# A linear-recurrence kernel (RWKV WKV): another timetable for the output stores, and one set of carry transfers on another queue

## Chip, cores and metric

The kernel runs on one core of a Trainium2 chip. The metric is the device time of one execution in microseconds (us); the median of three runs before the change is 285.42 us (284.81 to 285.78).

## What is computed

```python
for b in range(16):                      # batch; each of d_model = 256 channels on its own
    aa, bb, pp = 0, 0, -1e38
    for t in range(2048):
        ww = u + k[b, t]
        qq = maximum(pp, ww)
        e1, e2 = exp(pp - qq), exp(ww - qq)
        output[b, t] = (e1 * aa + e2 * v[b, t]) / (e1 * bb + e2 + 1e-08)
        ww = pp - w + k[b, t]
        qq = maximum(ww, k[b, t])
        e1, e2 = exp(ww - qq), exp(k[b, t] - qq)
        aa, bb, pp = e1 * aa + e2 * v[b, t], e1 * bb + e2, qq
```

A numerator and a denominator are carried along time with decay w, and each output is their quotient. Inputs k and v are 33.5 MB each, the output another 33.5 MB, all in 32-bit floats.

## The kernel before

Time is cut into 16 chunks of 128 steps, and the 16 batches into 4 groups of 4. A **tile** is one chunk of one group: 128 steps on the partitions, 4 x 256 channels along the free axis, 512 KB each of k, of v and of output. There are 64 tiles, numbered n = 4 c + p (chunk c, group p).

Within a tile the decayed sums are matrix products: the exponentials of k (two variants, one for each half of the recurrence) and their products with v lie in bf16 in a ring of 12 tiles, `EZR`, and TensorE multiplies them with triangular matrices: `den` (L357) makes the denominator, `num` (L375) the numerator. What a chunk inherits from the earlier ones is put into a row of each half of the tile, in the ring itself: these **carries** are worked out from sums over the chunk (`sums` to `state_next`, L250 to L333), turned by TensorE (`turn_back`, L336), copied to the small tile `cb` and written into the ring by four 8 KB transfers (`inject`, L343). `den` of the four tiles of a chunk can start only when its carries are in the ring.

The main loop goes through **slots**, n = 10 to 63 (after 10 slots that fill the pipeline). Slot n makes the exponentials of tile n, and for tile q = n - 10 the denominator and its reciprocal: ACT takes its logarithm into an output buffer (`den_log`, L363) and then exp of minus that (`den_exp`, L367). For the tile before, qp = n - 11, PE makes the numerators and DVE multiplies them in (`mult`, L379, two halves; the second is near the end of slot n). DVE also converts k (`round_k`, L190, of tile n + 2) and v (`cast_v`, L224) and multiplies exponentials with v (`times_v`, L231). After slot 63 a hand-written tail finishes tiles 53 to 63. Its first lines (L512 to L540) hold, in this order: `den(54)`, the stores that are left over, `den(55)`, the state of the last chunk, the store of tile 53, `den(56)` (the first that needs chunk 14's carries), `turn_back(15)`, and `inject(15)` on SyncE (SP). Then come tiles 54 to 63 one after the other; `den(60)` is the first that needs chunk 15's carries.

Every engine runs its instructions in the order in which they are written. SP issues all large transfers in such an order too: in each slot first `loads` (L79), usually v of one tile and k of the next, then `store` (L383) of as many tiles as the condition of L485 lets through. They share one hardware queue.

There are 19 data buffers of 512 KB, 8 of them for outputs at first. A list with due slots says which may be taken: a stored output's buffer is given back 4 slots after its store (`STORED`, L37, L386), which only sets the order; the real wait is a semaphore: `den_log` waits until the transfer that last read its buffer has landed. Where fewer than three output buffers are due, `loads` moves one over from the inputs (L81).

The condition in L485 gives, for tile m, a store in slot m + 14 up to slot 31, one slot later from 32, 44 and 56 on; from slot 59, when all is loaded, everything finished is stored at once (tiles 42 to 47 in that slot).

Carries go out on GpSimd's (POOL's) queue, except those of the last chunk, which SP issues.

Of the kernel before, what the change touches and what calls it, by code (L numbers as in the profile page):

```python
# [15 lines left out]
def kernel(  # L16
# [10 lines left out]
    PE, DVE, SC, POOL, SP = nc.tensor, nc.vector, nc.scalar, nc.gpsimd, nc.sync  # L27
# [4 lines left out]
    NST = T // TC  # L32
    D = 2 * Dm
    NP = 4 * NST
# [42 lines left out]
    loaded = 5  # L77

    def loads(slot):  # L79
        nonlocal loaded  # L80
        if slot + 2 >= LAG and sum(x <= slot + 2 for x, _ in free_out) < 3:  # L81
            free_out.append((slot + 2, take(slot, free)))
        while loaded < NP and loaded - slot < 9 and sum(x <= slot for x, _ in free) >= 2:
            load_v(loaded, slot)
            loaded += 1
            if loaded < NP:
                load_k(loaded, slot)
# [102 lines left out]
    def round_k(n, slot=0):  # L190
        km = consts.tile([128, 4, Dm], F32R, tag=f"km{n % 2}", name="km") if n < 2 else KM[n - 2]
        kr = kr_of.pop(n)
        K(DVE.tensor_copy(km, kr))  # L193
        free.append((slot, kr))
        KM[n] = km

    def logs(n):
        km = KM[n].rearrange("p (i n) d -> p i (n d)", i=2)

        def rows(q):  # L200
            for i in range(2):
                g = 32 * (2 * q + i)
                K(PE.matmul(half(n, q)[:, i, :], CO[g:g + 32, :],  # L203
                            WU[g:g + 32, :].unsqueeze(1).broadcast_to([32, 2, Dm]), start=True, stop=False,
                            tile_position=(g, 0), skip_group_check=True))

        def steps(q):
            for i in range(2):
                K(PE.matmul(half(n, q)[:, i, :], (NLE, NLZ)[q], km[:, i, :], start=False, stop=True,  # L209
                            skip_group_check=True))  # L210

        rows(0)
        rows(1)
        steps(0)
        steps(1)

    def exps(n):
        if n < TURNS:
            for q in range(2):
                K(SC.activation(ez(n)[:, q], half(n, q), ACT.Exp))  # L220
        else:
            K(SC.activation(ez(n)[:, 0:2], PS[:, 0:4, :].rearrange("p (q i) x -> p q i x", q=2), ACT.Exp))  # L222

    def cast_v(n, slot=0):  # L224
        vb = vbpool.tile([128, 4, Dm], BF16, tag="vb", name="vb")
        vr = vr_of.pop(n)
        K(DVE.tensor_copy(vb, vr))  # L227
        free.append((slot, vr))
        VB[n] = vb

    def times_v(n):  # L231
        vb = VB.pop(n).rearrange("p (i n) d -> p i (n d)", i=2)
        K(DVE.tensor_mul(ez(n)[:, 2:4], ez(n)[:, 0:2], vb.unsqueeze(1).broadcast_to([128, 2, 2, D])))  # L233
# [109 lines left out]
    def inject(c, queue=POOL):  # L343
        cb = small.tile([128, 128], BF16, tag="cb", name="cb")
        K(DVE.tensor_copy(cb, st.pop((c, "CT"))))  # L345
        r0 = 4 * c % RING
        for q in range(2):
            for h in range(2):
                r, x = HS * h + HS - 1, 32 * (2 * q + h)
                K(queue.dma_start(  # L350
                    out=EZR[r:r + 1, 2 * q, r0:r0 + 4, :, :].rearrange("o p i (b x) -> o (p i b) x", b=4),
                    in_=cb[x:x + 32, :]))
# [4 lines left out]
    def den(n, bank=DENB):  # L357
        for m, q in (("L", 0), ("Id", 1)):
            for i in range(2):
                K(PE.matmul(bank[:, i, :], mats[m], ez(n)[:, q, i, :], start=q == 0, stop=q == 1,  # L360
                            skip_group_check=True))
# [13 lines left out]
    def num(n, bank, i):  # L375
        for m, q in (("LN", 2), ("IdN", 3)):
            K(PE.matmul(bank, mats[m], ez(n)[:, q, i, :], start=q == 2, stop=q == 3, skip_group_check=True))  # L377

    def mult(n, bank, i):  # L379
        rd = RD[n]  # L380
        K(DVE.tensor_mul(rd[:, i, :], bank, rd[:, i, :]))  # L381

    def store(n, slot):  # L383
        rd = RD.pop(n).rearrange("p i (n d) -> p (i n) d", n=2)
        K(SP.dma_start(out=rows_of(out, n), in_=rd))
        free_out.append((slot + STORED, rd))  # L386

    later = {}
    for c in range(NST):
        s = 4 * c + 3  # L390
        plan = [(s + 1, "act" if s + 1 < LAG else "recip", copy_sums), (s + 1, "pe", turn),
                (s + 2, "act", state_logs), (s + 2, "mid", state_frames), (s + 2, "scan", state_scan), (s + 2, "scan", state_offsets),
                (s + 3, "recip", state_weights), (s + 3, "chain", state_chain),
                (s + 4, "nums", turn_back), (s + 4, "mid", inject), (s + 4, "mid", state_next)]
        if c == 0:
            plan = [(s + 1, "act", copy_sums), (s + 1, "pe", turn), (s + 1, "pe", state_logs),
                    (s + 1, "round", state_frames), (s + 1, "round", state_scan), (s + 1, "round", state_offsets),
                    (s + 2, "act", state_weights), (s + 2, "round", state_chain),
                    (s + 3, "pe", turn_back), (s + 3, "round", inject), (s + 3, "round", state_next)]
        if c == 1:  # L400
            plan = [(s + 1, "act", copy_sums), (s + 1, "pe", turn), (s + 2, "act", state_logs),
                    (s + 2, "round", state_frames), (s + 2, "round", state_scan), (s + 2, "round", state_offsets),
                    (s + 3, "recip", state_weights), (s + 3, "early", state_chain)] + plan[8:]
        if c == NST - 1:
            plan = []
        for slot, where, f in plan:
            later.setdefault((slot, where), []).append((f, c))

    def small_work(n, where):
        for f, c in later.pop((n, where), []):  # L410
            f(c)
# [35 lines left out]
    stored = 0  # L447

    def inverses(n):
        q, qp = n - LAG, n - LAG - 1  # L450
        if qp >= 0:
            num(qp, NUMB, 1)

        sums(n - 1)
        if n + 1 < NP:
            recip(q, lambda: small_work(n, "recip"))

    for n in range(LAG, NP):

        q, qp = n - LAG, n - LAG - 1  # L460
        if qp >= 0:
            num(qp, NUMB, 0)
        den(q)
        small_work(n, "nums")
        exps(n)
        small_work(n, "act")
        if qp >= 0:
            mult(qp, NUMB, 0)
        small_work(n, "mid")
        if n == LAG:  # L470

            inverses(n)
            small_work(n, "early")
        if n + 2 < NP:
            round_k(n + 2, n)

        if n % 4 in (3, 0):
            cast_v(n, n)
        if n + 1 == NP:
            times_v(n)  # L480
        elif n % 4 < 2:
            cast_v(n + 1, n)
        loads(n)

        while stored < (qp - 2 - max(0, n - 20) // 12 if loaded < NP else qp):  # L485
            store(stored, n)
            stored += 1
        if n > LAG:
            inverses(n)
        if qp >= 0:  # L490
            mult(qp, NUMB, 1)
        small_work(n, "scan")
        if n + 1 < NP:
            times_v(n)
            small_work(n, "chain")
            logs(n + 1)
        small_work(n, "pe")
# [4 lines left out]
    q, c = NP - LAG - 1, NST - 1  # L502
# [48 lines left out]
    n, p = NP - 1, (NP - 1) % 4  # L551
# [38 lines left out]
```

## Time and profile before

| | |
|---|---|
| time, median of 3 | 285.42 us |
| profiled span | 283.5 us |
| busy: DVE, PE, ACT, POOL | 261.1, 256.2, 253.6, 106.0 us |
| transfers | 67.12 MB read, 33.55 MB written |
| slot in the steady part | 15.9 us for 4 slots |
| 512 KB load or store, issue to landing | 8.0 to 8.2 us (median) |
| carry transfer of 8 KB, issue to landing | 5.3 us from POOL, 1.9 us from SP |

Read the page in three parts. Up to about 42 us the kernel fills its pipeline; up to about 254 us it runs the slots; then the tail. A high busy share over the whole span hides that: the parts have to be looked at one by one, and in each the question is which wait ends last.

### The profile page before, as it was taken

To read this page: it belongs to the slowest core of one execution; us is meant where nothing else is said; L and a number is where in the kernel's file an instruction comes from. 1 tells how busy PE (TensorE), PEld (TensorE's weight loads), DVE (VectorE), ACT (ScalarE), POOL (GpSimd) and SP (SyncE) were. 2 spreads that over 40 slices of the span, in tenths; PEclk is the share of its full clock that TensorE was granted. 3 is DMA by queue.
4 is the path that set the end of the run, shared out by engine and by line. 5 is a ranking of instruction groups with operands and counts; after the bars stand their busy time and mean duration, and the time that the engine had idled before them with its cause. 6 is when DMAs were issued, how large, how long until landed. Compare 5 with 4: busy or idle time off the path is not lost.

```text
span 283.5 us, 5049 instructions
## 1 busy us (share of the span) xinstructions
PE 256.2 (90%) x1662; PEld 119.5 (42%) x1694; DVE 261.1 (92%) x465; ACT 253.6 (89%) x252; POOL 106.0 (37%) x206
## 2 busy tenths in 40 slices
PE   6997896999999999999999999899999999997990
PEld 2444442544454444544454444444444344433430
DVE  4699989999999999999999999999999999987863
ACT  2576678999999999999999999899999999997991
POOL 7000424263445444253445445143546546242000
PEclk9999999999999999999999999999999999999997
DMA  6999999999999999999999999999999999999597
GB/s 225 349 348 350 348 331 350 333 348 352 384 375 382 384 381 385 383 382 382 384 377 384 375 384 377 378 376 369 382 379 384 383 384 378 380 384 334 167 340 252
DMA packets 103586, 101.54 MB, mean 358 GB/s; under 512 B 4284, under 2 KB 103560, under 8 KB 103560
## 3 DMA queue, kind: packets, MB, share of 16 engines
q1 hardware_dynamic: 101336, 100.45, 103.9%
q0 software_dynamic: 1920, 0.50, 0.8%
q8 instruction: 13, 0.21, 0.3%
q10 hardware_dynamic: 304, 0.27, 0.3%
q14 instruction: 13, 0.11, 0.1%
HBM read 67.12 MB, written 33.55 MB: 355 GB/s over the span
## 4 chain that ended last, share of the span: by engine, by line
DVE 35%; PE 27%; DMA 16%; ACT 9%; issue 9%; DVEq 1%; POOL 0%; ACTq 0%; POOLq 0%
DVE EZR L233 14%; DVE buf L381 11%; PE PS L377 9%; PE PS L209 9%; DMA buf<-in_k_dram 7%; DMA out_dram<-buf 6%; PE PS L257 3%; PE PS L203 3%; ACT EZR L222 3%; ACT buf L365 3%; DVE vb L227 3%; DVE km L193 3%; PE PS L360 2%; ACT buf L368 2%; DMA EZR<-cb 2%
## 5 line engine op out<-in xcount | busy, mean ns | idle before, releaser
L222 ACT ACTIVATE EZR<-PS 128x2048 bf16<-128x2048 f32 x54 | 101.2, 1874 | 3.3 <-PE PS L209 2.6
L381 DVE TENSOR_TENSOR buf<-PS,buf 128x512 f32<-128x512 f32 x128 | 87.6, 692 | 6.3 <-ACT buf L368 4.2
L233 DVE TENSOR_TENSOR EZR<-EZR,vb 128x2048 bf16<-128x2048 bf16 x64 | 78.3, 1224 | 3.1 <-ACT EZR L220 2.5
L365 ACT ACTIVATE buf<-PS 128x1024 f32<-128x1024 f32 x64 | 65.8, 1028 | 3.4 <-DMA out_dram<-buf 1.6
L368 ACT ACTIVATE buf<-buf 128x1024 f32<-128x1024 f32 (+1 forms) x65 | 67.9, 1049 | 0.9
L377 PE MATMUL PS<-EZR,LN 128*128 128x512 bf16 x128 | 48.8, 381 | 10.3 <-DVE buf L381 6.7
L350 POOL DMA_DIRECT2D EZR<-cb x60 | 36.7, 617 | 52.0 <-DVE cb L345 44.6
L209 PE MATMUL PS<-km,NLE 128*128 128x512 f32 x128 | 47.6, 454 | 1.8 <-DVE km L193 1.8
L193 DVE CAST km<-buf 128x1024 fp32r<-128x1024 f32 x64 | 44.2, 691 | 1.3 <-DMA buf<-in_k_dram 1.2
L227 DVE CAST vb<-buf 128x1024 bf16<-128x1024 f32 x64 | 43.3, 695 | 0.0
L377 PE MATMUL PS<-EZR,IdN 128*128 128x512 bf16 x112 | 42.4, 378 | 0.0
L209 PE MATMUL PS<-km,NLZ 128*128 128x512 f32 x128 | 41.0, 403 | 0.0
L360 PE MATMUL PS<-EZR,L 128*128 128x512 bf16 x128 | 38.1, 379 | 1.6 <-DMA EZR<-cb 1.6
L360 PE MATMUL PS<-EZR,Id 128*128 128x512 bf16 x115 | 35.3, 379 | 0.0
L288 POOL TENSOR_TENSOR F<-LL,LL 128x32 f32<-128x32 f32 x13 | 8.5, 654 | 63.6 <-ACT LL L279 63.6
L203 PE MATMUL PS<-WU,CO 32*128 32x512 bf16 x256 | 26.9, 393 | 2.7 <-DVE WU L421 1.6
L257 PE MATMUL PS<-EZR,OH 128*32 128x256 bf16 x512 | 26.2, 277 | 2.9 <-ACT LL L279 0.7
L209 PEld LDWEIGHTS PS<-km,NLZ 128*128 128x128 f32 x128 | 24.6, 192 | 5.7
L220 ACT ACTIVATE EZR<-PS 128x1024 bf16<-128x1024 f32 x20 | 19.4, 1020 | 8.4 <-PE PS L209 8.4
L209 PEld LDWEIGHTS PS<-km,NLE 128*128 128x128 f32 x128 | 19.4, 191 | 17.0 <-issue 12.9
L377 PEld LDWEIGHTS <-IdN 128*128 128x128 bf16 x128 | 12.5, 97 | 23.0 <-issue 20.8
L377 PEld LDWEIGHTS <-LN 128*128 128x128 bf16 x128 | 12.8, 100 | 18.3 <-issue 11.3
(71 smaller groups left out, 202.8 us busy)
## 6 DMA issues: line engine op xcount, KB each, us to landing
buf<-in_k_dram SPq DMA_DIRECT2D x64, 512.0 KB, 8.2
buf<-in_v_dram SPq DMA_DIRECT2D x64, 512.0 KB, 8.1
out_dram<-buf SPq DMA_DIRECT2D x63, 512.0 KB, 8.0
EZR<-cb POOLq DMA_DIRECT2D x60, 8.0 KB, 5.3
out_dram<-buf SPq DMA_DIRECT2D x2, 128.0 KB, 3.3
out_dram<-buf ACTq DMA_DIRECT2D x2, 128.0 KB, 3.2
EZR<-cb SPq DMA_DIRECT2D x4, 8.0 KB, 1.9
wuf<-in_w_dram ACTq DMA_DIRECT2D x1, 8.0 KB
```

Source lines behind the costliest of these rows:

```text
L193: K(DVE.tensor_copy(km, kr))
L203: K(PE.matmul(half(n, q)[:, i, :], CO[g:g + 32, :], WU[g:g + 32, :].unsqueeze(1).broadcast_to([32, 2, Dm]), start=True, stop=False, tile_p ...
L209: K(PE.matmul(half(n, q)[:, i, :], (NLE, NLZ)[q], km[:, i, :], start=False, stop=True, skip_group_check=True))
L222: K(SC.activation(ez(n)[:, 0:2], PS[:, 0:4, :].rearrange("p (q i) x -> p q i x", q=2), ACT.Exp))
L227: K(DVE.tensor_copy(vb, vr))
L233: K(DVE.tensor_mul(ez(n)[:, 2:4], ez(n)[:, 0:2], vb.unsqueeze(1).broadcast_to([128, 2, 2, D])))
L350: K(queue.dma_start(out=EZR[r:r + 1, 2 * q, r0:r0 + 4, :, :].rearrange("o p i (b x) -> o (p i b) x", b=4), in_=cb[x:x + 32, :]))
L360: K(PE.matmul(bank[:, i, :], mats[m], ez(n)[:, q, i, :], start=q == 0, stop=q == 1, skip_group_check=True))
L365: K(SC.activation(RD[n], bank, ACT.Ln, scale=RS))
L368: K(SC.activation(RD[n][:, i, :], RD[n][:, i, :], ACT.Exp, scale=-1.0))
L377: K(PE.matmul(bank, mats[m], ez(n)[:, q, i, :], start=q == 2, stop=q == 3, skip_group_check=True))
L381: K(DVE.tensor_mul(rd[:, i, :], bank, rd[:, i, :]))
```

## The change

```diff
-                (s + 4, "nums", turn_back), (s + 4, "mid", inject), (s + 4, "mid", state_next)]
+                (s + 4, "nums", turn_back), (s + 4, "mid", inject if c < NST - 2 else lambda c: inject(c, SP)),
+                (s + 4, "mid", state_next)]
...
-        while stored < (qp - 2 - max(0, n - 20) // 12 if loaded < NP else qp):
+        while stored < qp - (min(5, max(0, n - 18) // 5) if n < NP - 3 else 3):
             store(stored, n)
             stored += 1
```

The first edit concerns chunk 14 alone, the last that goes through this plan: its four carry transfers, in slot 63, are issued by SP and not by POOL. The second sets another timetable. Tile m is stored in slot m + 12, the first slot after its last `mult`, up to slot 22; from slots 23, 28, 33, 38 and 43 on each time one slot later, so from 43 on in slot m + 17. From slot 61 on the distance is m + 15. The buffers that outputs and loads use, and the points at which input buffers are moved over, follow from the new timetable. It is meant to give output buffers back in time, and to keep transfers that nothing waits for behind those that something waits for.

| stores | before | after |
|---|---|---|
| tile 0 | slot 14 | slot 12 |
| tile 10 | slot 24 | slot 22 |
| tile 15 | slot 29 | slot 29 |
| tile 25 | slot 40 | slot 41 |
| tile 39 | slot 55 | slot 56 |
| tiles 42 to 47 | slot 59 | slots 59 to 62 |
| tiles 48 to 51 | slots 60 to 63 | 48 in slot 63; 49 to 51 in the tail |

No instruction of PE, DVE or ACT is added, removed or moved; four transfer issues move from POOL to SP.

## The prediction

> **What bounds the kernel now.** I first read the page's slices and the chain by engine, to find the parts; then the windows, part by part; then the timeline around the waits.
>
> ```profile
> DVE  4699989999999999999999999999999999987863
> ACT  2576678999999999999999999899999999997991
> DMA  6999999999999999999999999999999999999597
> GB/s 225 349 348 350 348 331 350 333 348 352 384 375 382 384 381 385 383 382 382 384 377 384 375 384 377 378 376 369 382 379 384 383 384 378 380 384 334 167 340 252
> ...
> DVE 35%; PE 27%; DMA 16%; ACT 9%; issue 9%; DVEq 1%; POOL 0%; ACTq 0%; POOLq 0%
> ```
>
> One slice is 7.1 us. Up to slice 6 (42 us) transfers are full and DVE and ACT are not: loads bound the start. Then everything is full. Loads alone move at 349 GB/s, with stores among them at 380 to 384. From the issue list, two loads alone take 3.0 us, two loads with a store 4.1 us, against a slot of 3.97 us.
>
> ```profile
> core 0: us, PE busy (x) PEld busy (x) DVE busy (x) ACT busy (x) POOL busy (x), PEclk, DMA share, GB/s
> ...
> 119.00:135.00 16.00, 15.28 (x105) 7.24 (x106) 15.85 (x28) 15.82 (x16) 6.98 (x13) 1.00 1.09 382
> 135.00:151.00 16.00, 14.63 (x101) 6.82 (x101) 15.66 (x26) 15.19 (x15) 6.71 (x13) 1.00 1.09 381
> ...
> 167.00:183.00 16.00, 14.79 (x98) 6.84 (x99) 15.56 (x27) 15.20 (x16) 6.26 (x13) 1.00 1.09 378
> ...
> 262.50:269.00 6.50, 6.45 (x31) 2.96 (x31) 5.18 (x10) 6.50 (x8) 0.00 (x0) 1.00 0.48 157
> 269.00:283.50 14.50, 7.46 (x32) 2.96 (x31) 7.47 (x12) 8.27 (x10) 0.00 (x0) 0.88 0.88 298
> ```
>
> Up to 135 us DVE and ACT have under 0.2 us free in 16: they bound the slots, and a timetable of transfers can't speed them up. Between 135 and 199 us ACT loses some 0.6 us twice. The timeline of ACT names it: `den_log` waits for a store to give its buffer back.
>
> ```profile
> 142.29 1.03 ACT L365 ACTIVATE buf<-PS 128x1024 f32<-128x1024 f32 x1 [0.65 <-DMA out_dram<-buf]
> ...
> 178.50 1.03 ACT L365 ACTIVATE buf<-PS 128x1024 f32<-128x1024 f32 x1 [0.70 <-DMA out_dram<-buf]
> ```
>
> These are slots 35 and 44; smaller gaps lie before `den_log` in slots 34, 41, 45 and 49 (0.12, 0.22, 0.04, 0.22 us): 1.95 us on ACT in all. In the chain in order of time, `times_v` of equal slots starts at 122.35, 154.74 and 187.18 us; eight slots take 31.8 us undisturbed, so the path lost 0.59 and then 0.64 us. Then the tail:
>
> ```profile
> 253.95 2.05 POOL L350 DMA_DIRECT2D EZR<-cb  x4 [3.57 <-DVE cb L345]
> ...
> 260.10 0.59 PE L360 MATMUL PS<-EZR,L 128*128 128x512 bf16 x2 [1.55 <-DMA EZR<-cb]
> ...
> 261.16 1.02 ACT L365 ACTIVATE buf<-PS 128x1024 f32<-128x1024 f32 x1 [1.48 <-PE PS L360]
> ...
> 262.25 0.29 DVE L345 CAST cb<-PS 128x128 bf16<-128x128 f32 x1 [1.30 <-PE PS L339]
> ...
> 262.57 2.52 SPq L350 DMA_DIRECT2D EZR<-cb  x4
> ```
>
> POOL issues chunk 14's carries from 253.95 to 256.0, they land by about 260, and `den(56)`, ready at 258.55, waits 1.55 us. `turn_back(15)` and `inject(15)` queue behind it. From there ACT needs 1.86 us for a tile and sets the pace to the end. In 262.5 to 269 us transfers are half idle (157 GB/s): there is room there for stores that are put off.
>
> **What the Trainium skill says.** "DMA: Bandwidth & Descriptors", section "Queues, rings and completion order": a DMA engine takes one ring's descriptors in order and goes round-robin between rings. The trace agrees: SP's transfers land in the order of issue, 6.9 us after the end of issue when backlogged, and a small carry takes 5.3 us from POOL even beside that backlog, 1.9 us from SP with little in front. The same page, "Anatomy of one DMA": DMA engines do not wait on semaphores, the issuing sequencer does. So a waiting transfer on SP holds all that are written behind it; the trace shows SP still from 260.4 to 262.57 for `cb` of chunk 15. Its "Specifications" put the HBM limit per core at about 358 GB/s; the trace has 380 to 384 over most of the span, which I use.
>
> **The change, part by part.**
>
> *Stores two slots earlier, slots 12 to 22.* S0 now goes out behind v of tile 18 and k of tile 19, and ahead of all later loads; with two more stores in front these land 2.7 us later (2 x 1.37). What waits for them is `round_k`; k landed 5.9 to 7.6 us before its use for tiles 20 to 30, so at least 3.1 us stay. Cost nothing. ACT gains nothing either: no `den_log` waited before slot 34.
>
> *From slot 29 on* I count positions in SP's order, which with transfers always full give landing times. S15, S16 and S17 stand at the same positions as before (88, 91, 94), so the waits in slots 34 and 35 stay. Slot 36 took a former input buffer and now takes that of S18, three transfers after S17 (142.2 us): it lands at 142.2 + 3 x 1.4 = 146.4, against `den_log` at 146.07: a new wait of 0.4 us. In slots 44, 45 and 49 the buffers come from S24, S25 and S28, which land 4.1 to 4.5 us ahead of need: 0.96 us on ACT, 0.64 us on the path, is removed. The new wait in slot 36, part of it absorbed by the wait in 41, I put at 0.25 us by the same share (0.64/0.96 of 0.4). Sum: **0.4 us gained**. Loads there come as early or up to 3 us earlier; k's least reserve is 1.5 us (tile 62) before, and 1.9 (tile 60, same position) afterwards, less the 0.4: still positive.
>
> *Carries of chunk 14 on SP.* Before them SP has issued S47, at 248.75 us as now (same order up to it). `cb` is ready at 253.66 - 0.4 = 253.25, so SP stands 4.5 us and the queue, 6.9 us deep, is nearly empty when the carries go out. No page line has SP issue carries on a full ring; bounds are the 1.3 us from end of issue to landing for chunk 15's and the 5.3 us of POOL. I take 1.3: issued 253.3 to 255.8, landed 257.1, before `den(56)` is ready at 258.15. The 1.55 us wait is gone. But `turn_back(15)` needs `CB` from DVE, ready at 260.96; so it starts at 260.98 and not at 261.83, and `den(57)` behind it gains **0.85 us**. ACT follows at its 1.86 us a tile.
>
> *What is queued behind the carries on SP.* S48 to S52, which were issued 248.8 to 256.6. S48 now goes out at 256.3; a store alone takes 2.6 us from end of issue to landing (S54 before), so 258.9. Five more at 1.37 us (S42 to S52 landed 10 in 13.74 us): S53 lands at 265.8, `inject(15)` (issued by 263.7) just behind, at 266. `den(60)`, at 267.23 before, now wants it at 266.0: just in time. S54 to S62 then follow ACT; the last had 2.7 us from issue to landing, and the end moves by the compute's gain.
>
> Sum: 0.4 + 0.85 = 1.25 us, 285.42 - 1.25 = **284.2 us**.
>
> **The rivals.**
>
> *A, as above:* 284.2.
>
> *B, the put-off stores become the bound of the tail.* S54 to S62 landed every 1.54 us (268.33 to 280.68), not 1.37. At that rate S53 and with it `inject(15)` land at 266.6, and S62 nine stores later at 280.5, both halves of S63 at 282.0, against 282.18 before. Against it: S42 to S52, with more in flight, ran at 1.37. The tail then gains 0.2 us; with 0.4 from the slots: 284.8; with none from the slots 285.2.
>
> *C, all waits go.* If store landings come a little earlier in slots 34 to 36, since stores replaced loads in the queue early, the whole 1.23 us is saved, and 0.85 in the tail: 283.3. Against it: the positions are equal, and so are the counts of loads and stores up to there.
>
> *D, slower.* SP's in-order wait leaves DMA idle, and the same reserve that the early stores eat makes store landings around slot 35 later. If they are 0.7 us later (half a transfer), the waits in slots 33 to 36 grow by 0.7 + 0.4 and only 0.64 comes back: +0.5. If S48 lands a transfer later (260.3) and stores run at 1.54, S63 ends at 260.3 + 15 x 1.54 = 283.4, +1.2. Together 287.1, either alone 285.9 to 286.6. For it: stores at the full rate outrun the slot (4.1 against 3.97 us), so SP's lag only grows while the distance is short. Against it: the same transfers stand ahead of S15 in both.
>
> **How the numbers follow.** A 0.50, B 0.22, C 0.10, D 0.18. The predicted time is A's. The 0.3% bounds are 284.56 and 286.28. Faster: nearly all of A (0.45), C (0.10) and a little of B (0.05) make 0.60. Slower: half of D and its upper end, 0.12. Same: the rest, 0.28. The range runs from C, 283.3, to the lower part of D, 285.9.
>
> **What would show it.** Right: no idle time before `den_log` in slots 44 and 49, some 0.4 us in slot 36; `den(56)` without a wait, DVE's `cb` cast of chunk 15 waiting for `CB`'s product only; carries from SP landing within 2 us; a hole in the transfers near 256 us. Wrong: PE waiting at `den(60)` for carries (B); stores landing late up to the last (B, D); DVE waiting for k after 50 us, or longer waits in slots 33 to 36 (D).

## The result and the profile after

| | before | after |
|---|---|---|
| time, median | 285.42 us | 287.69 us (11 runs, 286.76 to 289.72) |
| ratio | 1 | 1.0078 (95%: 1.0052 to 1.0105) |
| profiled span | 283.5 us | 286.0 us |

The change costs 2.3 us, where the prediction had a gain of 1.2. These are the rows of the page after that answer to those shown of before: busy tenths of DVE and ACT, granted TensorE clock, transfers and their rate in 40 slices, now of 7.15 us each, and the chain by engine.

```profile
DVE  4698999999999999999999999999999999998553
ACT  2586588999999999998999999999999999998781
PEclk9599999999999999999999999999999999999988
DMA  5999999999999999999999999999999999969897
GB/s 194 358 348 351 349 333 348 332 359 378 385 380 383 380 382 377 379 381 373 384 366 370 374 382 385 376 384 378 374 383 377 376 379 380 369 212 320 271 340 250
...
DVE 39%; PE 25%; DMA 17%; issue 9%; ACT 8%; DVEq 1%; POOL 0%; SPq 0%; ACTq 0%; POOLq 0%
```

Up to slice 34 the rows are nearly those of before. Then the rate falls to 212 GB/s in slice 35 (250 to 257 us) and to 271 in slice 37, where DVE falls to 5 tenths. Before had one low slice, 167. Nearly all that changed lies in the tail: the exponentials of tile 63 start at 251.9 us before and at 252.2 after, and from there to the end it is 31.6 us before and 33.8 after. SP's own timeline there (start, duration, engine, line, transfer, count) says why:

```profile
254.08 2.52 SPq L350 DMA_DIRECT2D EZR<-cb  x4
256.65 6.86 SPq L385 DMA_DIRECT2D out_dram<-buf  x6
263.61 3.88 SPq L350 DMA_DIRECT2D EZR<-cb  x4
267.60 13.13 SPq L385 DMA_DIRECT2D out_dram<-buf  x9
```

S47's issue ends at 249.27 us. SP then stands until chunk 14's carries can go (254.08), needs 2.52 us to issue the four, and only then issues S48 to S53, before chunk 15's carries; S54 to S62 follow from 267.60 on. Two windows of before:

```profile
core 0: us, PE busy (x) PEld busy (x) DVE busy (x) ACT busy (x) POOL busy (x), PEclk, DMA share, GB/s
253.00:257.00 4.00, 3.65 (x32) 1.49 (x33) 3.75 (x7) 3.65 (x4) 2.70 (x6) 1.00 1.08 377
265.00:269.00 4.00, 4.00 (x21) 1.81 (x19) 2.75 (x5) 4.00 (x6) 0.00 (x0) 1.00 0.71 236
```

The windows of after:

```profile
core 0: us, PE busy (x) PEld busy (x) DVE busy (x) ACT busy (x) POOL busy (x), PEclk, DMA share, GB/s
247.00:253.00 6.00, 5.92 (x37) 2.77 (x34) 5.25 (x11) 5.97 (x7) 3.00 (x8) 1.00 1.09 385
253.00:257.00 4.00, 3.65 (x30) 1.21 (x29) 3.76 (x7) 3.97 (x4) 0.57 (x2) 1.00 0.33 111
257.00:261.00 4.00, 3.63 (x18) 1.72 (x18) 3.42 (x14) 3.38 (x7) 0.00 (x0) 1.00 0.83 270
265.00:269.00 4.00, 1.99 (x10) 0.77 (x9) 2.45 (x4) 3.34 (x4) 0.00 (x0) 1.00 0.66 218
269.00:273.00 4.00, 4.00 (x13) 1.55 (x14) 1.38 (x2) 1.97 (x2) 0.00 (x0) 0.66 1.02 339
```

A hole (111 GB/s) where 377 GB/s moved before, and PE only half busy from 265 to 269, where before had it busy throughout. The timeline of PE and ACT names what PE waits for; the bracket is the idle time before, and what ended it:

```profile
268.95 0.59 PE L360 MATMUL PS<-EZR,L 128*128 128x512 bf16 x2 [2.01 <-DMA EZR<-cb]
270.01 1.02 ACT L365 ACTIVATE buf<-PS 128x1024 f32<-128x1024 f32 x1 [1.67 <-PE PS L360]
271.06 1.06 PE L360 MATMUL PS<-EZR,L 128*128 128x512 bf16 x2
273.01 1.02 ACT L365 ACTIVATE buf<-PS 128x1024 f32<-128x1024 f32 x1 [1.03 <-PE PS L360]
```

`den(60)` waits 2.01 us for `inject(15)`, whose four transfers lie behind S48 to S53 in SP's queue and land at 268.65 to 269.13; it needs the first two, the second of which lands at 268.81. In this execution the TensorE clock is then halved for 3.4 us from 270.3 on (two matmuls of 512 columns take 1.06 us, not 0.59), and ACT loses 1.03 us more.

Working theory T: neither edit alone is slow. The timetable leaves SP with nothing to issue after S47, the carries' move puts an in-order wait there, and the put-off stores then delay `inject(15)`. Rivals: the timetable alone, or the carries on SP alone; or that the late stores bound the end whatever the carries do.

### The profile page after: what moved, and what is told of

Its sections match the earlier page's. It is cut to its first block, busy times and chain, and to the rows that moved or that the text cites. A ratio compares the mean times of both kernels' runs of the same rounds, so it can differ in the third digit from the quotient of the medians.

```text
span 286.0 us, 5052 instructions
## 1 busy us (share of the span) xinstructions
PE 257.8 (90%) x1662; PEld 120.3 (42%) x1694; DVE 261.5 (91%) x465; ACT 253.9 (89%) x252; POOL 101.9 (36%) x202
## 4 chain that ended last, share of the span: by engine, by line
DVE 39%; PE 25%; DMA 17%; issue 9%; ACT 8%; DVEq 1%; POOL 0%; SPq 0%; ACTq 0%; POOLq 0%
DVE EZR L233 15%; DVE buf L381 11%; PE PS L377 9%; PE PS L209 8%; DMA buf<-in_k_dram 8%; DMA out_dram<-buf 6%; DVE km L193 4%; DVE vb L227 3%; PE PS L257 3%; PE PS L203 3%; ACT EZR L222 2%; PE PS L360 2%; ACT buf L365 2%; ACT buf L368 2%; DMA wuf<-in_u_dram 2%
## 5 line engine op out<-in xcount | busy, mean ns | idle before, releaser
L350 POOL DMA_DIRECT2D EZR<-cb x56 | 34.7, 625 | 50.9 <-DVE cb L345 43.7
```

## Experiments

All ratios are to the kernel before, run on the same chip.

**One part at a time.** The timetable alone:

```diff
-  (s + 4, "mid", inject if c < NST - 2 else lambda c: inject(c, SP)),
+  (s + 4, "mid", inject),
```

> The new timetable of stores, with chunk 14's carries issued by POOL as before. Theory T (the loss lies in the pair: SP stands for cb of chunk 15-1 with the put-off stores behind it, and the last carries then queue behind these stores): SP does not stand, S48 to S52 go out by 256.6 us as before, den(56) waits some 1.5 us for POOL's carries as before, den(60) does not wait; 285.0 to 286.0 us, within 0.3% of before. Rival R1 (the timetable alone costs it: stores put off to the tail are too many for it): about 287.5 us, with a wait at den(60).

Measured: 285.33 us, ratio 0.9999 (0.9988 to 1.001). And the carries alone, with the timetable of before:

```diff
-  while stored < qp - (min(5, max(0, n - 18) // 5) if n < NP - 3 else 3):
+  while stored < (qp - 2 - max(0, n - 20) // 12 if loaded < NP else qp):
```

> The timetable of before, with chunk 14's carries issued by SP. Theory T: at that point SP has only just issued S50 (253.2 us), so it stands under 1 us, and the transfers have no hole; but the carries queue behind 5 stores and land at 259 to 260 us, so den(56) waits about as long as before and nothing is gained: 285.0 to 286.0 us. Rival R2 (four carries on SP cost their 2.5 us of issue time, whatever stands around them): 286.5 us or more, with S51 and S52 late and a wait at den(60).

Measured: 285.29 us, 0.9989 (0.9981 to 0.9998). Each part alone costs nothing; only the pair does. SP's timeline and `den(56)` of the carries-only kernel, then the window of the hole:

```profile
247.22 5.84 SPq L385 DMA_DIRECT2D out_dram<-buf  x4
254.52 3.08 SPq L350 DMA_DIRECT2D EZR<-cb  x4
257.69 3.46 SPq L385 DMA_DIRECT2D out_dram<-buf  x3
259.98 0.59 PE L360 MATMUL PS<-EZR,L 128*128 128x512 bf16 x2 [0.59 <-DMA EZR<-cb]
...
253.00:257.00 4.00, 3.79 (x32) 1.33 (x30) 3.86 (x8) 3.97 (x4) 0.67 (x2) 1.00 1.00 351
```

Here SP stands too, but S48 to S50 were issued ahead of the wait and keep the transfers at 351 GB/s. The carries land behind them at 259.7 to 260.8, so `den(56)` still waits 0.59 us. With the timetable alone POOL issues the carries and SP does not stop; `den(56)` then waits 1.30 us.

**A dose of the cause.** The changed kernel, with two of the put-off stores (S48, S49) ahead of chunk 14's carries, and then with one (S48):

```diff
-  ... if n < NP - 3 else 3):
+  ... if n < NP - 3 else 1):     # two ahead; 2 for one ahead
```

> The changed kernel, but from slot 61 on stores follow at a distance of m + 13, so that S48 and S49 go out in the time in which SP stood, ahead of chunk 14's carries; S50 to S53 stay behind them. Theory T: the transfers' hole shrinks from some 3.3 us to under 1, carries of chunk 14 land by 258.5 us and den(56) does not wait, S53 and the carries of chunk 15 land by 266.5 us and den(60) waits under 0.3 us: 284.3 to 285.2 us. Rival R1 (too much put off in the slots before): still over 287. Rival R2: over 286.5, as the four issues stand where they stood.

> The same with a distance of m + 14: S48 alone ahead of chunk 14's carries. Theory T: a hole of some 2 us, carries of chunk 15 at about 267.3 us, a wait of 0.3 to 1 us at den(60): 285.0 to 286.3 us, between the changed kernel and the one with two stores ahead. R1 and R2: no step between them, over 286.5 us.

| stores ahead of the carries | time | ratio (95%) | wait of `den(60)` |
|---|---|---|---|
| 0 (after; repeated) | 287.69; 287.32 | 1.0078; 1.0069 | 2.01; 1.53 us |
| 1 | 286.07 | 1.0017 (1.0003 to 1.0032) | 0.37 us |
| 2 | 285.01 | 0.9985 (0.997 to 0.9999) | 0 |

The time follows the number of stores that SP has issued when it comes to stand. One thing was not expected: with two ahead, `den(56)` still waits 0.62 us for the first set. SP's timeline with two ahead:

```profile
247.39 4.43 SPq L385 DMA_DIRECT2D out_dram<-buf  x3
253.05 3.29 SPq L350 DMA_DIRECT2D EZR<-cb  x4
256.43 3.53 SPq L385 DMA_DIRECT2D out_dram<-buf  x4
261.13 3.47 SPq L350 DMA_DIRECT2D EZR<-cb  x4
```

Four stores and not six stand between the two sets of carries, and the second set is issued by 264.6 us, in place of 267.5.

**Carries ahead of the stores.** Here S49 to S53 are issued after `inject(15)`.

```diff
-    for n in range(stored, q):
-        store(n, q + LAG)
...
-    store(q, q + LAG)
...
     inject(c, SP)
+    for n in range(stored, q + 1):
+        store(n, n + LAG)
```

> The changed kernel, with S49 to S53 issued after chunk 15's carries and not ahead of them. Theory T has two parts, late carries and a store queue that the hole has left too long for the tail: den(60) does not wait, but the stores of 49 to 63 start only at about 264 us and take 1.54 us each, so the last lands near 287.5 us; 288 to 290 us. Rival R3 (the whole loss is the wait at den(60), stores have room enough): 285.0 to 285.8 us, as the wait is gone.

Measured: 293.04 us, 1.0259 (1.0235 to 1.0284), above what was expected. The edit made a wait of its own:

```profile
267.30 1.02 ACT L365 ACTIVATE buf<-PS 128x1024 f32<-128x1024 f32 x1 [7.83 <-DMA out_dram<-buf]
268.38 1.01 PE L360 MATMUL PS<-EZR,L 128*128 128x512 bf16 x2 [5.47 <-ACT buf L365]
```

`den_log(56)` takes the buffer of a store that was put off again, and stands for 7.83 us. So this run doesn't part the carries' wait from the stores' lateness; the next two do.

**Without the second set.** The changed kernel, and as a control the kernel before, leave out the transfers of chunk 15's carries; the cast to `cb` stays.

```diff
-    inject(c, SP)
+    cb = small.tile([128, 128], BF16, tag="cb", name="cb")
+    K(DVE.tensor_copy(cb, st.pop((c, "CT"))))
```

> The changed kernel without the transfers of chunk 15's carries (their values are worked out and not written, so the outputs of the last chunk lack what earlier chunks hand on). den(60) then can't wait. Theory T (part of the loss is this wait, the rest the stores that the hole has delayed): 285.3 to 286.3 us, with the last stores landing one behind the other up to the end. Rival R3 (the wait is the whole loss): 284.5 us or less, as den(56) gains its 0.85 us. Rival R4 (the hole is the whole loss, the wait would have been hidden by stores anyway): 287.0 us or more, as the changed kernel.

> The kernel before without the transfers of chunk 15's carries, as a control: there they land some 0.8 us ahead of den(60), so that all theories expect no gain from the wait, and at most a few tenths from the 2.5 us of issue time on SP ahead of S54 to S56: 284.9 to 285.5 us.

> The changed kernel as it is, a second time on the chip of these runs, so that the two kernels without the last carries stand beside it: 287.2 to 288.2 us in all theories. Its profile also tells whether the wait at den(60) of 2 us and the halved TensorE clock after it come back.

| | ratio (95%) |
|---|---|
| after, repeated | 1.0069 (1.0044 to 1.0095) |
| after without chunk 15's carries | 1.0031 (1.0016 to 1.0046) |
| before without chunk 15's carries | 0.9996 (0.9985 to 1.0008) |

Before loses nothing to them. After loses 1.0069 - 1.0031 = 0.38% or 1.1 us to them, and 0.31% or 0.9 us to something else; with intervals of 0.15 to 0.25 points on each, that is a rough split. The edit takes away two things at once, the wait of `den(60)` and the 3.9 us in which SP issues the set ahead of S54. The windows of the kernel without the second set name the rest (its profiled execution is one of its longest, by what lies ahead of the tail, so only stretches within it are read):

```profile
257.00:261.00 4.00, 3.91 (x25) 1.73 (x24) 3.36 (x8) 3.38 (x5) 0.00 (x0) 1.00 0.38 119
265.00:269.00 4.00, 4.00 (x20) 1.86 (x19) 3.17 (x6) 4.00 (x5) 0.00 (x0) 1.00 1.04 343
273.00:277.00 4.00, 3.53 (x16) 1.54 (x16) 2.86 (x5) 4.00 (x6) 0.00 (x0) 1.00 1.04 340
```

The hole is there (119 GB/s), from 265 us on the transfers are always full at 340 to 343 GB/s, and ACT is full too. From the exponentials of tile 63 to the end of S62's issue this kernel takes 25.3 us (254.1 to 279.4), before took 26.1 (251.9 to 278.0): the compute did gain 0.8 us. But S62 lands 4.3 us after its issue, against 2.7 before. The end waits for stores, which the hole made late.

**What ends last.** The repeat of the changed kernel has `den(60)` waiting 1.53 us in its profile, without any halved clock. (The profile puts this wait down to ACT, but it ends 0.13 us after the second carry has landed, and the one of 2.01 us ends 0.14 us after.) So the computation of the repeat is 1.9 us ahead in the tail, and the end comes only 0.4 us sooner. All times here are counted from the start of the exponentials of tile 63, one profiled execution each:

| | issue of S62 ends | S62 has landed | end |
|---|---|---|---|
| before | 26.1 us | 28.8 | 31.6 |
| after | 28.5 | 31.1 | 33.8 |
| after, repeated | 26.6 | 31.0 | 33.4 |
| after without chunk 15's carries | 25.3 | 29.6 | 32.4 |
| one store ahead | 25.4 | 29.8 | 32.0 |
| two stores ahead | 25.3 | 29.4 | 31.6 |

In the repeat S62 lands 4.4 us after its issue, where a store alone takes 2.6: the computation has 1.8 us to spare there, and by this reading the wait of `den(60)`, 1.53 us, costs that execution nothing. In the first execution wait and halved clock delay the computation by so much that it ends together with the stores: from S54 to S60 these land every 1.53 us, which for S62 gives 270.75 + 8 x 1.53 = 283.0, and it landed at 283.35. So the third rival of the beginning is right in its first half: late stores bound the end. But it does depend on the carries.

The second set of carries makes them later once more. In the changed kernel DVE has finished tiles 54 and 55 at 264.47 us, but their stores go out only from 267.60 on, when SP has issued the four carries:

```profile
262.00 2.47 DVE L381 TENSOR_TENSOR buf<-PS,buf 128x512 f32<-128x512 f32 x4
```

Meanwhile the transfers run dry a second time: 218 GB/s from 265 to 269 us (216 in the repeat), against 343 in the kernel without the set. The traces show this order; no run takes away the wait of `den(60)` and leaves SP's issue of the set, or the other way about.

**A shorter issue.** In the two-ahead kernel, and then in the changed kernel itself, SP writes a set of carries as two transfers of 16 KB, not four of 8 KB:

```diff
+        if queue is SP:
+            for q in range(2):
+                K(queue.dma_start(
+                    out=EZR[HS - 1:TC:HS, 2 * q, r0:r0 + 4, :, :].rearrange("h p i (b x) -> h (p i b) x", b=4),
+                    in_=cb[64 * q:64 * q + 64, :]))
+            return
```

> The kernel with two stores ahead of chunk 14's carries, where SP writes the carries of chunks 14 and 15 in two transfers each and not four. If the 2.5 us that SP takes to issue four carries hold up the stores behind them, S50 and S54 go out some 1.2 us earlier and the end, which waits for stores there, moves by 0.4 to 1 us: 284.0 to 284.7 us. Rival (the carries' own landing is the limit): each of the larger transfers lands later, den(56) waits over 1 us, 285 us or more.

> The changed kernel with chunk 14's and chunk 15's carries in two transfers each and not four; no store goes ahead of them. If the hole is priced by its length (SP stands for cb, then issues the carries for 2.5 us, and only then S48), S48 goes out 1.2 us earlier, the carries of chunk 15 land about 1.2 us earlier or more, and the wait at den(60) falls from 1.5 to 2 us to under 0.8: 286.0 to 286.7 us, between the changed kernel and the one with one store ahead. If only what stands ahead of the carries counts, 287.2 us or more, as the changed kernel.

With two ahead: 284.71 us, 0.9974 (0.9959 to 0.9988). In the changed kernel, with no store ahead: 285.19 us, 0.9982 (0.9969 to 0.9995). That is below what was expected; only the first set's saving had been counted. SP's timeline, `den(60)` and the hole of that last kernel:

```profile
253.72 1.27 SPq L349 DMA_DIRECT2D EZR<-cb  x2
255.04 6.61 SPq L391 DMA_DIRECT2D out_dram<-buf  x6
261.82 2.41 SPq L349 DMA_DIRECT2D EZR<-cb  x2
266.97 0.61 PE L366 MATMUL PS<-EZR,L 128*128 128x512 bf16 x2 [0.40 <-DMA EZR<-cb]
...
253.00:257.00 4.00, 3.66 (x32) 1.49 (x33) 3.75 (x7) 3.63 (x4) 0.29 (x1) 1.00 0.54 177
```

The first set takes 1.27 us to issue, not 2.52. The second takes 2.41, not 3.88: behind six stores a carry takes SP 1.0 to 1.2 us, against 0.63 on an emptier ring. The hole is smaller, the wait 0.40 us and not 2.01. So issue time on SP was itself part of the loss, ahead of S48 and ahead of S54.

**Buffers, and both.** In the two-ahead kernel an output buffer is given back one slot later (an older store's buffer is taken); and that together with the two-transfer carries:

```diff
-    STORED = 4
+    STORED = 5
```

> The kernel with two stores ahead of chunk 14's carries, and output buffers given back five slots after their store and not four (more buffers then go over from inputs to outputs). If waits of den_log for buffers hold up the slots, they are gone here, at the price of k landing later: no idle time of ACT before den_log in slots 33 to 49, k still lands before its use; 0.2 to 0.9 us below the kernel with four slots, 284.2 to 284.9 us. Rival (the queue of transfers is the limit, so that waits only change their place): DVE waits for k or the tail waits for stores, and the time stays at 285.0 us within 0.3.

> Both of these: five slots, and two transfers for the carries. If both act, and each where it is said to, their gains add: 283.6 to 284.6 us. If the queue of transfers is the limit all along, 284.6 to 285.2 us.

Five slots: 285.01 us, 0.9988 (0.9971 to 1.0006), nothing gained. Both: **283.83 us, 0.9956 (0.9933 to 0.9979)**, faster than both kernels. SP's timeline in it:

```profile
246.92 4.42 SPq L391 DMA_DIRECT2D out_dram<-buf  x3
253.08 1.27 SPq L349 DMA_DIRECT2D EZR<-cb  x2
254.46 5.25 SPq L391 DMA_DIRECT2D out_dram<-buf  x4
261.15 1.19 SPq L349 DMA_DIRECT2D EZR<-cb  x2
...
253.00:257.00 4.00, 3.91 (x31) 1.55 (x30) 3.50 (x6) 3.35 (x6) 0.00 (x0) 1.00 1.04 358
```

No hole (358 GB/s), no `den` waits for carries, and S62 lands 2.6 us after its issue, as a store alone does; in the two-ahead kernel it took 4.1. Why both together gain more than the sum of each is not settled: its interval reaches just to that sum. In the profiles the tail takes 30.5 us with two transfers alone and with both, so that the difference lies ahead of it, or in the spread of the executions.

## Why the prediction was wrong

**The early stores** cost nothing, as argued: the timetable alone is at 0.9999.

**The slots.** The waits in slots 44, 45 and 49 went, and slot 36 got one of 0.22 us (0.4 was forecast). The gain of 0.4 us did not come, because slot 33 now waits:

```profile
134.78 1.03 ACT L365 ACTIVATE buf<-PS 128x1024 f32<-128x1024 f32 x1 [0.99 <-DMA out_dram<-buf]
...
146.96 1.03 ACT L365 ACTIVATE buf<-PS 128x1024 f32<-128x1024 f32 x1 [0.22 <-DMA out_dram<-buf]
```

S15 landed at 134.7 us, against 133.5 before, though it stands at the same position in SP's queue. All gaps before `den_log` in slots 33 to 49 sum to 1.68 us after and 1.95 before, of which 0.27 and 0.22, in slot 41, end with a product of PE and not with a store. The step treated one execution's landing times as fixed. In nine of the 14 profiles, of either timetable, no such wait is longer than 0.2 us. In six of the nine the clock had been low near 47 us and the exponentials of slot 28 came 1.0 to 3.3 us later than before, so that stores had more time; in the other three, the repeat of the changed kernel among them, they came within 0.4 us of before, and why these three wait so little is open. In that repeat S15 lands 1.7 us after the exponentials of slot 33 begin, in the first execution 3.0 us. A wait of half a microsecond for a store is a matter of the execution here, and no sum of such waits in one trace is a forecast.

**Carries of chunk 14 from SP.** Right. `den(56)` no longer waits, and the cast to `cb` waits 0.49 us, for PE's product only:

```profile
261.79 0.29 DVE L345 CAST cb<-PS 128x128 bf16<-128x128 f32 x1 [0.49 <-PE PS L339]
```

The compute gain of 0.85 us is borne out by the 0.8 us of the kernel without the second set.

**What is queued behind them.** This is the step that failed. It followed S48 to S53 and chunk 15's carries down to `den(60)` "just in time"; three of its terms were too small, and it had no slack to lose:

| term | taken | measured |
|---|---|---|
| S48 has left SP | 256.3 us | 257.2 |
| from there to S48's landing | 2.6 us | 4.6 |
| five more stores, S49 to S53 | 5 x 1.37 = 6.9 us | about 6.6 (at 1.33 or so each) |
| chunk 15's carries issued | 2.5 us | 3.9 |
| `inject(15)` landed | 266.0 us | 269.1 |
| S62 landed | 280.68 - 1.25 = 279.4 us | 283.35 |

The first term is late because computation was 0.8 us later than assumed (`cb` at 254.08, not 253.25). The second is the largest: 2.6 us is what a store alone takes, with nothing else in the ring. The Trainium skill, "DMA: Bandwidth & Descriptors", section "Anatomy of one DMA — SWDGE (gpsimd) path", gives a transfer on GpSimd's path a fixed cost of some 2 us and the rest by bytes, at 436 GB/s. An estimate by that page is 3.2 us for 512 KB; SP's lone store took 2.6 here, and neither figure fits S48, which had four carries in front, others behind, and landed 4.6 us after its issue (4.1 in the repeat, 2.6 with two-transfer carries). The time per store was not at fault up to S53. The carries' issue was priced from a set on an emptier ring. It did not hold up `den(60)`, which needs the first two carries: these were issued by 266.22 and landed at 268.81, 2.6 us later, where a carry with little in front takes 1.3. So S53 just ahead (landed about 268.5) held them. What the long issue held up is S54.

The last row is the part of the step that decides. It let S54 to S62 follow ACT and moved the end by the compute's gain. But S54 landed at 270.75 us, 2.4 us later than before (268.33), and from there the stores themselves set the pace: the compute's gain of 0.8 us, which the kernels with stores ahead have too (25.3 us against 26.1), can't reach the end.

Rivals B and D had this bound, and B also "PE waiting at `den(60)` for carries". B's rate, 1.54 us a store, is what the tail ran at once it was full (340 GB/s), but B took S48's landing over from the first case. D had S48 one transfer late (260.3 us, measured 261.8), and its "283.4" for the last landing was the right kind of sum from too early a start. From 261.8 that sum gives 284.9, and 284.85 was measured; so close a fit is partly luck, since the first stores came every 1.33 us and a gap followed, when SP issued chunk 15's carries. No rival had that second gap.

**The halved clock** was in no rival. The Trainium skill, "TensorE: Matmul & The Clock Gate", section "Part 1: The HAM clock gate (the "warmup" mystery)", says that TensorE falls to half its clock after an idle window of some 3.4 us, that the windows run free of the program, and that the effect so varies between runs. The trace has the half clock for 3.4 us, but after a wait of only 2.01 us; in the repeat, after 1.53 us, it does not come. At the end the two executions differ by 0.4 us (33.8 and 33.4 us of tail), so that most of the loss is there without it. It may add more in others: the changed kernel's two slowest executions, 289.7 us, have a mean clock of 0.966 and 0.972, where the median of its 11 is 0.977, and 0.984 in 41 executions of the kernel before. No run isolates its share.

## What to carry to other kernels

When a transfer with a semaphore wait moves to a queue that carries bulk traffic, ask what that queue has already issued when it comes to stand, and what stands behind it: two transfers issued ahead bridged the wait here, none cost 2 us. Putting off "unimportant" stores is not free when something urgent is queued behind them later, nor when they still have to land before the end. A step that comes out "just in time" should be priced for being late. A wait that stands out in a trace need not be what the time is lost to: compare two executions, or ask how long the last transfer took from issue to landing. Count transfers on such a queue as well as bytes: two issues in place of four gave back the whole loss.

## What was not expected of the hardware

- A carry of 8 KB takes SP 0.63 us to issue with little outstanding (2.52 us for four), and 0.97 with six 512 KB stores just ahead (3.88 for four).
- After an idle stretch, stores run at 339 to 343 GB/s (273 to 277 us in the kernel without the second set), where the stream at 247 to 253 us moves 385. The same is seen before, at 340 in the slice from 269 us on. Why is open.
- The TensorE clock is halved for 3.4 to 6.8 us near 47 us in 6 of 14 profiles, whichever timetable they have. The window from 46 to 50 us of the carries-only kernel, with a clock of 0.68, shows ACT at 1.82 us of 4, where before had 2.73 at full clock:

```profile
46.00:50.00 4.00, 3.73 (x20) 1.80 (x20) 3.36 (x6) 1.82 (x3) 2.86 (x6) 0.68 1.10 349
```
